# Norm scales made with tokens on partitions and turned by TensorE, wide squares in the gate stages, and a late residual scale

## The chip, the cores and the metric

The kernel runs on one core of one Trainium2 chip. A core has five engines with queues of their own: TensorE (PE in the rows; its weight loads are PEld), VectorE (DVE), ScalarE (ACT), GpSimd (POOL) and SyncE (SP), which here issues the weight transfers. Each works through its own instructions in order and waits on semaphores for the others. The metric is the device time of one execution in microseconds; lower is better.

## The reference, cut to what matters

One call computes two blocks on 256 tokens of width 1024. The first is ffn1, a mixer of two kinds of attention, ffn2 and a final norm. The second has two layers: SSD or retention, then PEER (a lookup among 16384 experts), then a gated embedding ("ple"), and a final norm. What the change touches is the norm in front of each stage; the first block's last norm and the second block's first stand directly one behind the other:

```python
def rms_norm(x, g):
    xf = x.astype(jnp.float32)
    y = xf * lax.rsqrt(jnp.mean(xf * xf, axis=-1, keepdims=True) + EPS)
    return (y * g.astype(jnp.float32)).astype(x.dtype)
...
    return rms_norm(x, final_norm)          # end of the first block
...
    h = x                                   # second block
    for i in range(DEPTH_2):
        hn = rms_norm_2(h, mix_norm[i])
        y = ssd_mixer(hn, ...) if i == 0 else retention(hn, ...)
        h = h + y
        h = h + peer_ffn(rms_norm_2(h, ffn_norm[i]), ...)
        g = jax.nn.sigmoid(rms_norm_2(h, ple_norm[i]) @ ple_gate[i])
        h = h + g * (p[i] @ ple_proj[i])
    return rms_norm_2(h, final_norm)
```

## The kernel before

The activations `x` lie feature-major in SBUF: 128 features on partitions, 8 chunks, 256 tokens. Every large product is made in three matmuls of split fp32 (L323 to L325: high weight by high and by low activation, low weight by high activation). A weight unit of 128x1024 is fetched by a SyncE transfer (L243) into one of three `w` buffers, cast by ScalarE to `wh` (L258) and subtracted by VectorE to `wl` (L260); the transfer for a unit three further on can start when that subtract has freed the buffer. There are three pairs of `wh` and `wl`, and two more are lent in some stages. The products go to four PSUM banks named `mm`, so TensorE can be at most four blocks ahead of whoever reads them.

A norm is made late: the products are taken of the unnormed `x` times its gain (`prep`, L353), and the result of each block is multiplied by `r`, one over the root of the mean square. For each chunk `prep` has ScalarE square `x` (L372) and GpSimd add it into `sqa` (L373). `root` (L401) sums over the partitions with one fp32 matmul of a ones matrix by `sqa` (L405), which leaves the sum on all 128 partitions for 256 tokens; ScalarE takes the root of 128x256 (L407) and `rstd` has VectorE make the reciprocal of 128x256 (L413). Where tokens are on partitions instead (the mixer's and the retention's values), `columns` (L416) turns a row of `r` with two small transposes (L421) and copies it (L423). `scales` (L380) already made such scales with tokens on partitions, for other norms, by one-column matmuls (L387), and `spread` (L394) turned them back with two transposes (L398).

The order on each engine is set by a scheduler from the order of the code. What is wrapped in `later` (L426) is made when first asked for, with a priority of 200 instructions ahead; `blocks` (L475) calls the consumer of a block's bank one block later with the same priority.

At the end of ffn2 two scales are made: `r1` for the first block's last norm, and `r2` for the second block's first norm on top of it, from `sqa` and from `sqb`, the squares times that norm's gain (`both`, L1443; `both_scales`, L1453). SSD's first products are multiplied by `r2` (`cv`, L837). The residual `x` itself must be multiplied by `r1` (L440, eight chunks) before SSD's output is added to it; `settle` (L1458) does so in steps that `ssd` calls between blocks. In the gate stages (`ple`, L1297) the squares come from a loop ahead of it, eight ScalarE squares and seven GpSimd adds.

The stages by the span's microseconds: ffn1 to 196, mixer to 321, ffn2 to 500, SSD to 711, peer0 to 1505, ple0 to 1547, retention to 1745, peer1 to 2539, ple1 to 2574, then the final norm.

## Time and profile before

| | |
|---|---|
| time, median of 3 runs (lowest to highest) | 2590.43 us (2588.69 to 2594.27) |
| the profiled execution | 2587.22 us |
| its span, first to last instruction | 2585.5 us |
| mean granted TensorE clock | 0.993 of full |
| busy: TensorE, VectorE, ScalarE, GpSimd | 98%, 77%, 52%, 7% of the span |

A timeline row gives the start, the time and the engine of one instruction or of a few alike in a row, its line, what it writes and reads, and in brackets how long the engine was idle before it and what ended that. A matmul row counts the records of the profiler: an fp32 matmul leaves two. Matmuls overlap, so the time between the starts of two rows tells what one costs, not the time of a row.

### The profile page before, as it was taken

What the parts mean: (1) busy time and instruction counts of PE and PEld (TensorE: products, weight loads), DVE (VectorE), ACT (ScalarE), POOL (GpSimd) and SP (SyncE); (2) the same over time, 40 slices, a digit from 0 to 9 for tenths busy, and PEclk for the clock granted to TensorE, in tenths of its full rate; (3) what the DMA queues carried; (4) which work ended last, traced back from release to release, by engine and by line L of the source; (5) the groups of instructions that cost most, each with busy time, mean ns of one, the idle gap of its engine ahead of it and who ended that gap; (6) DMA issues with size and microseconds to landing.
All of it is one profiled execution on the core that took longest, in us unless ns stands there. A gap on an engine that the chain in (4) does not pass through costs nothing.

```text
span 2585.5 us, 49071 instructions
## 1 busy us (share of the span) xinstructions
PE 2527.7 (98%) x19798; PEld 2349.4 (91%) x19798; DVE 1991.9 (77%) x3465; ACT 1337.3 (52%) x1824; POOL 191.6 (7%) x216
## 2 busy tenths in 40 slices
PE   8999999998999999999999999999999999999998
PEld 8998899988999999998888889999999999888887
DVE  8766776699789998868865566658999886886555
ACT  6555655587555444444444465555544444444445
POOL 1010100100102120000000030010112000000002
PEclk9999999999999999999999999999999999999999
DMA  6664366654465655555566656555565555556663
GB/s 219 203 193 140 123 197 188 184 204 142 133 192 184 199 180 165 167 176 179 170 189 192 195 182 188 165 167 187 185 194 182 165 167 176 179 171 190 192 193 122
DMA packets 128037, 460.20 MB, mean 178 GB/s; under 512 B 14688, under 2 KB 15424, under 8 KB 127168
## 3 DMA queue, kind: packets, MB, share of 16 engines
q1 hardware_dynamic: 125984, 452.32, 55.8%
q0 software_dynamic: 1536, 4.20, 0.5%
q8 instruction: 155, 2.54, 0.4%
q14 instruction: 74, 0.61, 0.1%
q10 hardware_dynamic: 288, 0.53, 0.1%
HBM read 455.91 MB, written 1.08 MB: 177 GB/s over the span
## 4 chain that ended last, share of the span: by engine, by line
PE 76%; DVE 7%; ACT 2%; issue 1%; POOL 1%; DMA 0%; POOLq 0%; DVEq 0%; ACTq 0%
PE mm L323 14%; PE mm L324 14%; PE mm L325 14%; PE acc L324 9%; PE acc L323 9%; PE acc L325 9%; PE mm L1119 2%; DVE wl L260 2%; DVE eq L1270 1%; DVE f L1273 1%; DVE ca L841 1%; PE pv L325 1%; PE pv L323 1%; PE pv L324 1%; PE sc L1240 1%
## 5 line engine op out<-in xcount | busy, mean ns | idle before, releaser
L258 ACT CAST wh<-w 128x1024 fp32r<-128x1024 f32 x856 | 889.9, 1041 | 1127.7 <-PE mm L324 544.4
L260 DVE TENSOR_TENSOR wl<-w,wh 128x1024 fp32r<-128x1024 f32 x856 | 1047.6, 1225 | 421.5 <-ACT wh L258 419.5
L323 PE MATMUL mm<-ah,wh 128*128 128x256 f32 x3448 | 967.0, 281 | 22.8 <-DVE cv L837 13.8
L325 PE MATMUL mm<-ah,wl 128*128 128x256 f32 x3448 | 962.0, 279 | 8.9 <-DVE wl L260 8.8
L324 PE MATMUL mm<-ah,wh 128*128 128x256 f32 x3448 | 962.7, 279 | 0.4 <-DVE ah L360 0.3
L323 PEld LDWEIGHTS mm<-ah,wh 128*128 128x128 f32 x3448 | 651.2, 189 | 26.2 <-issue 7.5
L325 PEld LDWEIGHTS mm<-ah,wl 128*128 128x128 f32 x3448 | 651.3, 189 | 14.4 <-DVE wl L260 13.9
L324 PEld LDWEIGHTS mm<-ah,wh 128*128 128x128 f32 x3448 | 651.8, 189 | 1.5 <-DVE ah L360 0.8
L324 PE MATMUL acc<-wl,ah 128*128 128x512 f32 x1024 | 402.8, 393 | 0.0
L325 PE MATMUL acc<-wh,ah 128*128 128x512 f32 x1024 | 398.6, 390 | 0.0
L323 PE MATMUL acc<-wh,ah 128*128 128x512 f32 x1024 | 307.0, 391 | 0.0
L323 PEld LDWEIGHTS acc<-wh,ah 128*128 128x128 f32 x1024 | 192.3, 188 | 39.5
L325 PEld LDWEIGHTS acc<-wh,ah 128*128 128x128 f32 x1024 | 192.2, 188 | 38.6
L324 PEld LDWEIGHTS acc<-wl,ah 128*128 128x128 f32 x1024 | 192.5, 188 | 38.2
L373 POOL TENSOR_TENSOR sqa<-sqa,sqt 128x256 f32<-128x256 f32 x82 | 82.7, 1009 | 1669.8 <-ACT sqt L372 1578.4
L1123 DVE TENSOR_TENSOR G<-mm,G 128x512 f32<-128x512 f32 x128 | 88.0, 689 | 49.8 <-PE mm L1119 49.8
L323 PE MATMUL mm<-hh,wh 128*128 128x256 f32 x352 | 97.2, 276 | 0.0
L324 PE MATMUL mm<-hl,wh 128*128 128x256 f32 x352 | 97.2, 276 | 0.0
L325 PE MATMUL mm<-hh,wl 128*128 128x256 f32 x352 | 97.2, 276 | 0.0
L1119 PEld LDWEIGHTS <-two 128*128 128x128 f16 x2048 | 69.8, 97 | 20.2 <-issue 15.9
L1107 DVE TENSOR_TENSOR two<-iota,tabs 128x1024 f16<-128x1024 f16 x128 | 87.3, 682 | 0.0
L1119 PE MATMUL mm<-one,two 128*128 128x64 f16 x2048 | 86.1, 194 | 0.0
(347 smaller groups left out, 3195.7 us busy)
## 6 DMA issues: line engine op xcount, KB each, us to landing
w<-in_peer_u_dram SPq DMA_DIRECT2D x256, 512.0 KB, 3.7
w<-in_peer_v_dram SPq DMA_DIRECT2D x256, 512.0 KB, 4.2
w<-in_ffn_gu_dram SPq DMA_DIRECT2D x88, 512.0 KB, 4.4
w<-in_ssd_in_dram SPq DMA_DIRECT2D x40, 512.0 KB, 4.1
w<-in_ffn_dn_dram SPq DMA_DIRECT2D x32, 512.0 KB, 3.7
w<-in_peer_q_dram SPq DMA_DIRECT2D x32, 512.0 KB, 4.3
w<-in_ssd_out_dram SPq DMA_DIRECT2D x16, 512.0 KB, 3.8
w<-in_ple_g_dram SPq DMA_DIRECT2D x16, 512.0 KB, 3.7
```

Of the source, the lines that this page charges most:

```text
L258: nc.scalar.copy(h[:, :n], w[:, :n])
L260: (nc.gpsimd if own else nc.vector).tensor_tensor(l[:, :n], w[:, :n], h[:, :n].bitcast(FT), OP.subtract)
L323: mm(ps, h, xh, start=start, stop=False, skip_group_check=True)
L324: mm(ps, h, xl, start=False, stop=False, skip_group_check=True)
L325: mm(ps, l, xh, start=False, stop=stop, skip_group_check=True)
L373: (add or nc.gpsimd).tensor_tensor(self.sq[tag], self.sq[tag], t, OP.add)
L841: nc.vector.scalar_tensor_tensor(acc[:, j:], v[:, :S - j], tap(3 - j), acc[:, j:], op0=OP.mult, op1=OP.add)
L1107: nc.vector.tensor_tensor(two, keys.to_broadcast(every), tab[1].to_broadcast(every), OP.is_equal)
L1119: nc.tensor.matmul(ps[:, t, :], two[:, t // 2, :, t % 2], one[i][:, t // 2, :, t % 2], start=i == 0, stop=i == 1)
L1123: nc.vector.tensor_tensor(ga, ps.rearrange("p t e -> p e t"), ga, OP.mult)
L1240: nc.tensor.matmul(ps[:, c * PK:(c + 1) * PK], qT[:, 2 * h + c, t * P:(t + 1) * P], keys[:, c, :], start=True, stop=True)
L1270: nc.vector.tensor_tensor(eq, f[:, c, h, :, None].to_broadcast([P, K, K]), self.iota[:, None, :K].to_broadcast([P, K, K]), OP.is_equal)
```

## The change

`rstd` now takes one or more tiles of squares. For each half of 128 tokens it multiplies the squares, as the stationary operand, by one column of ones, adding the tiles up in PSUM, so that the sums lie with tokens on partitions, two columns wide. Root and reciprocal are taken of 128x2; two transposes spread the result over the other half of the same bank, and VectorE copies 128x256 of it to `r`. The 128x2 tile is kept as `self.rt`, and `columns` is gone. `prep`'s last square is no longer added by GpSimd: it is kept as a second tile ("tail"), so a norm at the mixer, ffn2, peer and the retention has two tiles. In `both` the last chunk's two adds go to VectorE. `r1` is made by `settle`, inside SSD. The gate stage makes its own squares: two ScalarE squares of four chunks each, and two VectorE adds that leave two tiles; its blocks are consumed two later and not one later.

```diff
--- before.py
+++ after.py
@@ -359,9 +359,9 @@
         nc.scalar.activation(h, x, AF.Identity, scale=gc)
         nc.vector.scalar_tensor_tensor(l, x, gc, h.bitcast(FT), op0=OP.mult, op1=OP.subtract)
         if squares:
-            self.square(x, c == 0)
-
-    def square(self, x, first, tag="sqa", scale=1.0, add=None):
+            self.square(x, c == 0, tail=c == KC - 1)
+
+    def square(self, x, first, tag="sqa", scale=1.0, add=None, tail=False):
 
         nc = self.nc
         if first:
@@ -370,6 +370,9 @@
         else:
             t = self.small.tile([P, S], FT, tag="sqt", name="sqt")
             nc.scalar.activation(t, x, AF.Square, scale=scale)
+            if tail:
+                self.sq["tail"] = t
+                return
             (add or nc.gpsimd).tensor_tensor(self.sq[tag], self.sq[tag], t, OP.add)
 
     def near_sqrt(self, after):
@@ -398,30 +401,25 @@
             self.nc.tensor.transpose(ps[:, t * P:(t + 1) * P], c[:, t:t + 1].to_broadcast([P, P]), self.ident)
         return ps[:, :S]
 
-    def root(self, n, sq="sqa", eps=0, tag="r", bank="mm"):
+    def rstd(self, n, *sq, eps=0, tag="r", bank="mm"):
+
 
         nc = self.nc
         ps = self.bank(bank)
-        nc.tensor.matmul(ps[:, :S], self.ones, self.sq[sq], start=True, stop=True)
+        sq = sq or [self.sq[k] for k in ("sqa", "tail") if k in self.sq]
+        self.sq.pop("tail", None)
+        for t in range(NT):
+            for i, q in enumerate(sq):
+                nc.tensor.matmul(ps[:, t:t + 1], q[:, t * P:(t + 1) * P], self.ones[:, 0:1],
+                                 start=i == 0, stop=i == len(sq) - 1)
+        self.rt = c = self.small.tile([P, NT], FT, tag="cols", name="cols")
+        nc.scalar.activation(c, ps[:, :NT], AF.Sqrt, bias=self.vec("eps", eps), scale=1.0 / n)
+        nc.vector.reciprocal(c, c)
+        for t in range(NT):
+            nc.tensor.transpose(ps[:, S + t * P:S + (t + 1) * P], c[:, t:t + 1].to_broadcast([P, P]), self.ident)
         r = self.small.tile([P, S], FT, tag=tag, name=tag)
-        nc.scalar.activation(r, ps[:, :S], AF.Sqrt, bias=self.vec("eps", eps), scale=1.0 / n)
+        nc.vector.tensor_copy(r, ps[:, S:])
         return r
-
-    def rstd(self, *args, **keys):
-
-        r = self.root(*args, **keys)
-        self.nc.vector.reciprocal(r, r)
-        return r
-
-    def columns(self, r):
-
-        nc = self.nc
-        ps = self.bank()
-        for t in range(NT):
-            nc.tensor.transpose(ps[:, t:t + 1], r[0:1, t * P:(t + 1) * P], self.ident[0:1, 0:1])
-        c = self.small.tile([P, NT], FT, tag="cols", name="cols")
-        nc.vector.tensor_copy(c, ps[:, :NT])
-        return c
 
     def later(self, make):
 
@@ -662,7 +660,8 @@
                     for t in range(NT):
                         o = slice(t * P, (t + 1) * P)
                         self.mm3(pv[t], self.xh[:, k, o], self.xl[:, k, o], h[:, w], l[:, w], k == 0, k == KC - 1)
-            rt = self.columns(r())
+            r()
+            rt = self.rt
             mv = [pool.tile([P, 512], FT, name=f"mv{t}") for t in range(NT)]
             for t in range(NT):
                 nc.scalar.activation(mv[t], pv[t], AF.Identity, scale=rt[:, t:t + 1])
@@ -977,7 +976,7 @@
             decay = pool.tile([P, RET_H, NT, S], FT, name="decay")
             nc.sync.dma_start(decay, self.a["ret_decay"])
             turn = self.later(lambda: nc.vector.tensor_tensor(rot, rot, r()[:, None, :].to_broadcast([P, 2, S]), OP.mult))
-            rt = self.later(lambda: self.columns(r()))
+            rt = lambda: r() and self.rt
             yh, yl = pool.tile([P, 16, S], FR, name="yh"), pool.tile([P, 16, S], FR, name="yl")
 
             def rotated(name):
@@ -1294,9 +1293,17 @@
 
 
 
-    def ple(self, l, r, proj, ready):
+    def ple(self, l, proj, ready):
         nc, ws = self.nc, self.ws
         with self.tc.tile_pool(name="ple", bufs=2) as pool:
+            sq = pool.tile([P, KC, S], FT, name="sq", bufs=1)
+            for c in (0, 4):
+                nc.scalar.activation(sq[:, c:c + 4, :], self.x[:, c:c + 4, :], AF.Square)
+            self.near_sqrt(self.x[:, KC - 1, 0:1])
+            for c in (4, 2):
+                nc.vector.tensor_tensor(sq[:, :c, :], sq[:, :c, :], sq[:, c:2 * c, :], OP.add)
+            r = self.later(lambda: self.rstd(D, sq[:, 0, :], sq[:, 1, :]))
+
             def use(d, ps):
                 t = pool.tile([P, S], FT, name="t")
                 nc.vector.tensor_tensor(t, ps[:, :S], r(), OP.mult)
@@ -1309,7 +1316,7 @@
                 ready(d)
 
             ws.pool_every = 0
-            self.blocks(KC, use)
+            self.blocks(KC, use, lag=2)
             ws.pool_every = 0
 
 
@@ -1443,8 +1450,10 @@
             def both(d):
                 if d == 3:
                     self.near_sqrt(self.x[:, d, 0:1])
-                self.prep(d, "final_norm_both")
-                self.square(self.x[:, d, :], d == 0, "sqb", self.vec("final_norm", d))
+                add = nc.vector if d == KC - 1 else None
+                self.prep(d, "final_norm_both", squares=False)
+                self.square(self.x[:, d, :], d == 0, add=add)
+                self.square(self.x[:, d, :], d == 0, "sqb", self.vec("final_norm", d), add)
 
             more = ExitStack()
             pool = more.enter_context(tc.tile_pool(name="both", bufs=1))
@@ -1453,18 +1462,16 @@
             def both_scales():
 
                 nc.vector.scalar_tensor_tensor(sqb, self.sq["sqa"], EPS, sqb, op0=OP.mult, op1=OP.add)
-                return self.rstd(D, "sqb", 1, "r2"), self.root(D, bank="po")
+                return self.rstd(D, sqb, eps=1, tag="r2")
 
             def settle():
-                r1 = two()[1]
-                nc.vector.reciprocal(r1, r1)
+                r1 = self.rstd(D, bank="po")
                 yield
                 for c in range(0, KC, 2):
                     self.scale_residual("final_norm", r1, (c, c + 1))
                     yield
 
-            two = self.later(both_scales)
-            r = lambda: two()[0]
+            r = self.later(both_scales)
             for l in range(2):
                 if l == 0:
                     self.phase_banks(sc=2, po=2)
@@ -1482,16 +1489,12 @@
                 r = self.later(lambda: self.rstd(D))
                 self.phase_banks(sc=4)
                 proj = self.peer(l, r, f"ffn_norm_2{l}", lambda d: self.prep(d, f"ple_norm_2{l}", squares=False))
-                for c in range(KC):
-                    self.square(self.x[:, c, :], c == 0)
-                self.near_sqrt(self.x[:, KC - 1, 0:1])
-                r = self.later(lambda: self.rstd(D))
                 spare = self.lend((self.peer_at + [len(self.ws.units)])[l + 1])
                 if l == 0:
                     more = ExitStack()
                     pool = more.enter_context(tc.tile_pool(name="xparts2", bufs=1))
                     parts = [pool.tile([P, KC, S], FR, name=n) for n in ("bh", "bl")]
-                    self.ple(l, r, proj, lambda d: self.prep(d, f"mix_norm_2{l + 1}", parts))
+                    self.ple(l, proj, lambda d: self.prep(d, f"mix_norm_2{l + 1}", parts))
                     self.xh, self.xl = parts
                     r = self.later(lambda: self.rstd(D))
                 else:
@@ -1505,7 +1508,7 @@
                         if d < 3:
                             nc.scalar.activation(x, x, AF.Identity, scale=self.vec("final_norm_2", d))
 
-                    self.ple(l, r, proj, last)
+                    self.ple(l, proj, last)
             spare.close()
             c = self.scales(D, "sqa", "last")
             two = self.spread(c), self.spread(c)
```

VectorE at the start of SSD, before, from the sum for `r2` to the first product scaled by it (`wl` is a weight subtract, `x` the residual's scaling, `cv` the first reader of an SSD bank):

```order
L1455 SCALAR_TENSOR_TENSOR sqb<-sqa,sqb 128x256
L1460 RECIPROCAL r<-r 128x256
L260 TENSOR_TENSOR wl<-w,wh 128x1024
L440 SCALAR_TENSOR_TENSOR x<-x,vecs,r 128x256
L260 TENSOR_TENSOR wl<-w,wh 128x1024
L440 SCALAR_TENSOR_TENSOR x<-x,vecs,r 128x256 x5
L413 RECIPROCAL r_6294<-r_6294 128x256
L440 SCALAR_TENSOR_TENSOR x<-x,vecs,r 128x256 x2
L260 TENSOR_TENSOR wl<-w,wh 128x1024 x2
L837 TENSOR_TENSOR cv<-mm,r_6294 128x256
```

and the same place after:

```order
L376 TENSOR_TENSOR sqa<-sqa,sqt 128x256
L376 TENSOR_TENSOR sqb<-sqb,sqt 128x256
L1464 SCALAR_TENSOR_TENSOR sqb<-sqa,sqb 128x256
L260 TENSOR_TENSOR wl<-w,wh 128x1024 x2
L417 RECIPROCAL cols<-cols 128x2
L421 COPY r_6312<-mm 128x256
L260 TENSOR_TENSOR wl<-w,wh 128x1024
L836 TENSOR_TENSOR cv<-mm,r_6312 128x256
```

The residual's eight scalings and one weight subtract have moved from in front of the first `cv` to some 80 rows behind it, and the last square's two adds have come in.

ScalarE in ple0, before, from a weight cast (`wh`) through the last squares (`sqt`) to the norm's root:

```order
L258 CAST wh<-w 128x1024
L378 ACT_TABLE_LOAD
L378 ACTIVATE warm<-x,vecs 128x1
L372 ACTIVATE sqt<-x 128x256
L258 CAST wh<-w 128x1024
L372 ACTIVATE sqt<-x 128x256
L258 CAST wh<-w 128x1024
L372 ACTIVATE sqt<-x 128x256 x2
L258 CAST wh<-w 128x1024
L372 ACTIVATE sqt<-x 128x256
L258 CAST wh<-w 128x1024
L407 ACTIVATE r<-mm,vecs 128x256
```

and after:

```order
L258 CAST wh<-w 128x1024
L1301 ACTIVATE sq<-x 128x1024
L381 ACT_TABLE_LOAD
L381 ACTIVATE warm<-x,vecs 128x1
L258 CAST wh<-w 128x1024 x4
L416 ACTIVATE cols<-mm,vecs 128x2
L258 CAST wh<-w 128x1024
```

The squares are done four casts ahead of the root, and the root stands behind those casts.

VectorE in ple0, before, from `prep`'s last rows (`ah`) to the first block scaled by `r`:

```order
L360 SCALAR_TENSOR_TENSOR ah<-x,vecs,ah 128x256 x4
L260 TENSOR_TENSOR wl<-w,wh 128x1024
L360 SCALAR_TENSOR_TENSOR ah<-x,vecs,ah 128x256 x4
L260 TENSOR_TENSOR wl<-w,wh 128x1024 x5
L413 RECIPROCAL r<-r 128x256
L1302 TENSOR_TENSOR t<-mm,r 128x256 x2
```

and after:

```order
L360 SCALAR_TENSOR_TENSOR ah<-x,vecs,ah 128x256 x4
L260 TENSOR_TENSOR wl<-w,wh 128x1024
L1304 TENSOR_TENSOR sq<-sq 128x1024
L260 TENSOR_TENSOR wl<-w,wh 128x1024
L1304 TENSOR_TENSOR sq<-sq 128x512
L260 TENSOR_TENSOR wl<-w,wh 128x1024 x3
L417 RECIPROCAL cols<-cols 128x2
L260 TENSOR_TENSOR wl<-w,wh 128x1024
L421 COPY r<-mm 128x256
L1309 TENSOR_TENSOR t<-mm,r 128x256 x2
```

The adds have come in between the subtracts, and the copy of `r` stands one subtract behind the reciprocal. On TensorE, L405 stood after 48 of the stage's 192 matmuls; after, in ple0, the one-column matmuls stand after 71 and the transposes after 72, in ple1 after 61 and 72.

## Rows read from the trace of the kernel before

**Rows 1.** Page, first part: TensorE's busy time, share of the span, instructions.

```profile
PE 2527.7 (98%) x19798; PEld 2349.4 (91%) x19798; DVE 1991.9 (77%) x3465; ACT 1337.3 (52%) x1824; POOL 191.6 (7%) x216
```

**Rows 2.** TensorE's waits: us in total, times, longest us.

```profile
PE mm L323 <- DVE cv L837: 13.8, 5, 5.4
...
PE mm L405 <- POOL sqa L373: 7.7, 2, 4.4
...
PE po L889 <- DVE y L893: 4.1, 1, 4.1
```

**Rows 3.** Windows: stretch, length, busy us of PE, PEld, DVE, ACT, POOL, clock, DMA.

```profile
513.00:517.00 4.00, 3.90 (x18) 3.90 (x19) 3.23 (x11) 3.82 (x8) 0.00 (x0) 0.50 0.64 247
517.00:521.00 4.00, 4.00 (x32) 4.00 (x32) 2.03 (x6) 3.96 (x6) 0.00 (x0) 0.85 0.00 0
600.00:620.00 20.00, 16.72 (x148) 16.05 (x147) 19.95 (x41) 17.58 (x36) 0.00 (x0) 1.00 0.60 184
```

**Rows 4.** Timeline of TensorE round an L405 (start us, us, engine, line, operation).

```profile
500.48 0.28 PE L325 MATMUL mm<-ah,wl 128*32 128x256 f32 x1
500.60 0.59 PE L405 MATMUL po<-sqa,ones 128*128 128x256 f32 x2
...
501.15 0.28 PE L325 MATMUL mm<-ah,wl 128*128 128x256 f32 x1
```

**Rows 5.** Timeline of TensorE round one-column matmuls L387.

```profile
240.70 0.28 PE L324 MATMUL mm<-ah,wh 128*128 128x256 f32 x1
240.82 0.50 PE L387 MATMUL po<-ones,sqq 128*128 128x1 f32 x4
...
241.39 0.28 PE L323 MATMUL mm<-ah,wh 128*128 128x256 f32 x1
```

**Rows 6.** Timeline of TensorE round the transposes L398.

```profile
582.94 0.28 PE L325 MATMUL mm<-ah,wl 128*128 128x256 f32 x1
583.06 0.38 PE L398 MATMUL sc<-ident,col 128*128 128x128 f32 x2
...
583.40 0.28 PE L324 MATMUL mm<-ah,wh 128*128 128x256 f32 x1
```

**Rows 7.** Timeline of TensorE round the small transposes L421.

```profile
224.09 0.39 PE L325 MATMUL sc<-wh,ah 128*128 128x512 f32 x1
224.41 0.28 PE L421 MATMUL mm<-ident,r 1*128 1x1 f32 x2
...
224.84 0.28 PE L324 MATMUL mm<-ah,wh 128*128 128x256 f32 x1
```

**Rows 8.** Timeline of VectorE at the start of SSD.

```profile
503.41 1.16 DVE L260 TENSOR_TENSOR wl<-w,wh 128x1024 fp32r<-128x1024 f32 x1
...
506.02 2.06 DVE L440 SCALAR_TENSOR_TENSOR x<-x,vecs,r 128x256 f32<-128x256 f32 x5
508.00 1.74 DVE L413 RECIPROCAL r<-r 128x256 f32<-128x256 f32 x1
...
512.63 0.41 DVE L837 TENSOR_TENSOR cv<-mm,r 128x256 f32<-128x256 f32 x1
```

**Rows 9.** Timeline of ScalarE at the start of SSD.

```profile
504.90 1.05 ACT L258 CAST wh<-w 128x1024 fp32r<-128x1024 f32 x1 [0.93 <-PE mm L324]
```

**Rows 10.** Timeline of ScalarE in ple0.

```profile
1512.73 1.28 ACT L378 ACT_TABLE_LOAD   x1
...
1521.47 1.04 ACT L258 CAST wh<-w 128x1024 fp32r<-128x1024 f32 x1 [0.65 <-DMA w<-in_ple_g_dram]
```

**Rows 11.** Timeline of TensorE in ple0 and ple1, at the norm's matmul.

```profile
1522.40 1.22 PE L405 MATMUL mm<-sqa,ones 128*128 128x256 f32 x2 [4.40 <-POOL sqa L373]
1523.06 0.78 PE L323 MATMUL mm<-ah,wh 128*128 128x256 f32 x1
...
2555.00 0.70 PE L405 MATMUL mm<-sqa,ones 128*128 128x256 f32 x2 [3.33 <-POOL sqa L373]
```

**Rows 12.** Timeline of VectorE in ple0.

```profile
1515.60 1.25 DVE L260 TENSOR_TENSOR wl<-w,wh 128x1024 fp32r<-128x1024 f32 x1 [0.42 <-ACT wh L258]
```

## The prediction

> **What bounds the kernel now.** I read the page's first part, then the TensorE's list of waits, then the timelines at the longest of these waits. TensorE is busy 98% of the span [rows 1], so outside a few stretches any instruction added to TensorE costs its issue time and work taken from other engines costs nothing. The exceptions stand in the list of waits [rows 2]: 13.8 us for the first consumers of SSD's matmul banks (VectorE's `cv`, the longest 5.4), 7.7 in two waits of the norm's L405 for GpSimd's last square, and 4.1 for SSD's `y`. In the middle of SSD, from 600 to 620, VectorE is busy 19.95 of 20 us [rows 3]: there, and only there, VectorE sets the time. So the change can win in SSD and in the two gate stages (ple0 near 1520 us, ple1 near 2553), and must pay everywhere else.
>
> **Part 1: norm scales with tokens on partitions (all sites).** Before, a norm costs TensorE one ones-by-squares matmul. From the L325 at 500.48 to the one at 501.15 is 0.67 us and holds two ordinary steps of 0.113: L405 adds 0.44 [rows 4]. After, it is a one-column matmul per token tile and square tile and then two transposes. Both forms exist already. Four one-column records make 0.69 of two ordinary steps: +0.46 [rows 5]. Two transposes make 0.46 of two steps: +0.23 [rows 6]. The kernel's entry to ffn1 has one square tile (0.46 + 0.23 - 0.44 = +0.25). The entries to the mixer, ffn2, peer0, the retention and peer1 have two, `sqa` and the unadded last square: 2 x 0.46 + 0.23 - 0.44 = +0.71 each, 5 x 0.71 = +3.55. TensorE has no wait of note at these five, so GpSimd's last add and VectorE's 1.7 us reciprocal, both removed, hid behind queued matmuls; removing them saves nothing there. The dropped `columns` had two small transposes at two sites. From the L325 at 224.09 to the L324 at 224.84 is 0.75 for steps worth 0.33 [rows 7]: -0.42 each, -0.84 together. The new small steps stand in queues. At the mixer, VectorE's copy of `r` follows two weight subtracts of 1.2 us [rows 8] while TensorE has 14 matmuls (1.6 us) until it needs a bank; I add 0.4 for the mixer and peer0 together (bounds 0 and 1). Sum of part 1: 0.25 + 3.55 - 0.84 + 0.4 = **+3.4**.
>
> The Trainium skill ("TensorE: Matmul & The Clock Gate", section "Back-to-back issue gap") would price the one-column matmul lower: about 60 cycles for up to 64 columns, some 25 ns, when it stands alone. By it the five sites would cost 5 x (0.2 + 0.23 - 0.44), about nothing, and the forecast would be 3.6 us lower. The row decides against it: 0.46 us for four records, each of which has a 128-column weight load to itself.
>
> **Part 2: SSD's start and the late residual scale.** Before, VectorE runs a reciprocal for `r1`, six scalings L440 between weight subtracts, a second reciprocal of 1.74 us at 508.00, two scalings and two subtracts, and reaches the first `cv` at 512.63 [rows 8]. TensorE has run out of banks 5.4 us earlier and restarts at half clock: 513 to 517 is granted 0.50 and holds 18 matmuls where 35 fit [rows 3], some 2.5 us with the edges. So 8 us of TensorE's time hang on that `cv`. After, in front of it stand three 128x256 adds, three subtracts instead of four, a 128x2 reciprocal and one copy. The third subtract decides: its cast waits for TensorE to free a buffer, as it did at 504.90 before [rows 9]; TensorE comes there some 0.4 earlier without `r1`'s L405, so cast to 505.5, subtract to 506.7, `cv` near 506.7. That is 6.0 us earlier and before the banks run out; this stall and its half clock go.
>
> Part of it is given back, because the middle of SSD is VectorE's. Work that stood ahead of the first `cv` now stands behind: eight scalings (5 in 2.06 us [rows 8], 3.2), `r1`'s small reciprocal and copy (0.5) and one subtract (1.2), in all 4.9. Against that, VectorE waited for the half-speed TensorE behind `cv`: it was busy 3.23 and 2.03 of the four microseconds from 513 and from 517 [rows 3], so 2.7 us idle, which go with the half clock. Net at the end of SSD: -6.0 + 4.9 - 2.7 = -3.8. ScalarE gets a Sqrt table load and a reload inside SSD (1.28 each [rows 10]). ScalarE is not the bound there, but its `zt` and `ct` feed VectorE. Bounds: all 8 gained; or, with both loads in VectorE's way, -6.0 + 4.9 + 2.6 = +1.5. I take **-3.8**, nearest to the row that shows VectorE full.
>
> **Part 3: the gates' squares.** Before, seven GpSimd adds follow one another, TensorE issues two blocks (48 matmuls) and waits 4.40 us at L405, until 1522.40. It restarts at 1523.06 with 144 matmuls left, at half clock: the L405 pair took 1.22 us, against 0.59 at 500.60 [rows 4, 11]. After, two wide squares and two VectorE adds, estimated by casts and subtracts of that width, have the sum ready near 1518.4, and L413 stands after 71 matmuls. But the transposes stand one matmul later and need the reciprocal. ScalarE's Sqrt is behind four weight casts, where only one cast came between the last squares and the Sqrt before; the fourth is the trouble. Its buffer is refilled when the subtract three units earlier is over. Before, such a subtract ended at 1516.85 and the cast waiting for that DMA began at 1521.47, 4.6 us later [rows 10, 12]. After, a 128x1024 add stands in front of that subtract, so it ends near 1517.8, the cast runs from 1522.0 to 1523.0 and the Sqrt follows. Then VectorE does a subtract, the reciprocal, another subtract that waits for its own DMA, and only then the copy that frees the bank: near 1526.1 (subtracts of 1.2 us and, for the second, a refill that began near 1519.6). So the stall is not removed but moved, from 1517.9 to 1522.4 before, to 1520.9 to 1526.1 after. TensorE restarts 3.05 us later with 24 matmuls fewer (2.72), and at half clock again: **+0.5** (bounds: -3.5 if the Sqrt comes before the transposes are reached, and +2). In ple1 the order is alike, with 72 matmuls before the transposes. TensorE restarted at about 2555.3 before [rows 11]; the same chain of refill, cast, Sqrt, subtract, reciprocal, subtract, copy ends near 2559.5, 4.2 later for 2.7 fewer: **+1.6** (bounds -2 and +3).
>
> **Sum.** 3.4 - 3.8 + 0.5 + 1.6 = +1.7 us against the profiled execution, 2587.22 (span 2585.5 and 1.7 around it): 2588.9. The profiled one lies 3.2 below the median of the three runs, 2590.43; on the median's scale, 2592.1. What a measurement here can tell from no change is about 0.2%, 5.2 us.
>
> **Rivals.**
>
> A. The gate stalls close. If the refills land a little earlier than I count, the Sqrt is done before TensorE reaches the transposes: ple0 -3.5, ple1 -2. For it: the sum is ready almost two microseconds before TensorE asks for it, and GpSimd's chain is gone. Against it: the cast order, in which one late DMA holds the Sqrt. With my SSD term this is 3.4 - 3.8 - 3.5 - 2 = -5.9, 2584.5; with SSD's whole 8 us, 2580.3.
>
> B. SSD gives everything back, slower. Its place is VectorE's full stretch in the middle of SSD: 4.9 us of moved work and two table loads in ScalarE's queue ahead of VectorE's operands. It decides as soon as these cost more than the 6.0 us by which `cv` is earlier. The price is -6.0 + 4.9 + 2.6 = +1.5 in place of -3.8; with the gates as I have them 3.4 + 1.5 + 0.5 + 1.6 = +7.0, 2597.4, and with the gates at their upper bounds 2600.3. For it: 19.95 of 20 us. Against it: the idle behind `cv` at half clock, which must shrink.
>
> C. The small matmuls cost what the page says and not what the row says: 2588.5. It changes no sign; 2 in 100.
>
> D. The change does not do what it says, since `cv` still comes after the banks run out: the third subtract then waits for a weight that lands later, near 508 as before. Then 2 to 3 us of the stall and the half clock stay, SSD is about 0, and the time is 2595.9; 8 in 100.
>
> **How the numbers follow.** My forecast has 48 in 100, C 2, D 8, A 22, B 20. Forecast, C and most of D lie within 0.2% (2585.2 to 2595.6), with some edge on both sides. Faster: A and 4 of the forecast's edge, 0.26. Slower: B, half of D and a little edge, 0.26. Same: 0.48. The likeliest is 2592.1, its own range 2588 to 2596. The range for 8 in 10 goes half into A and half into B: 2582.5 to 2599.
>
> **What will show it.** Right: the first `cv` between 506 and 507.5 with no TensorE wait of over 1 us in front; the list of waits without L405's GpSimd waits but with L419 or the next matmul waiting 4 to 6 us in each gate stage, ended by a reciprocal or the copy of `r`; five places with about 0.7 us more on TensorE; and SSD's end 3 to 5 us earlier against its start. Wrong: a gate stage without a wait of over 2 us (A); SSD no shorter although the stall at 507 is gone (B); `cv` after 508 (D). My forecast also falls if the change lengthens the transfer waits elsewhere, which I count at nothing because the weight stream's order outside these stages is the same.

## The result

The changed kernel takes 2610.01 us (median of 4 runs, 2607.61 to 2612.04) against 2589.56 for the kernel before, run beside it: a ratio of 1.0076 [1.0058, 1.0093]. It is slower by 20 us, outside the predicted range. The profiled execution took 2608.58 us, with a span of 2606.8 against 2585.5: 21.3 us to find.

The page of the changed kernel, its span and its first part (busy us, share, instructions), against [rows 1]:

```profile
span 2606.8 us, 49173 instructions
PE 2546.6 (98%) x19862; PEld 2367.6 (91%) x19862; DVE 1985.1 (76%) x3479; ACT 1334.5 (51%) x1812; POOL 168.7 (6%) x195
```

TensorE is busy 19 us longer. So most of the loss isn't waiting, and the list of TensorE's waits in the changed kernel (us in total, times, longest), which answers to [rows 2], agrees:

```profile
PE mm L325 <- DVE wl L260: 8.5, 18, 1.0
PE mm L323 <- DVE r L421: 7.7, 4, 2.7
...
PE mm L323 <- DVE cv L836: 5.8, 3, 3.2
PE sc L875 <- DVE bc L844: 5.7, 2, 3.1
PE mm L419 <- DVE cols L417: 3.7, 2, 2.3
PE po L888 <- DVE e L884: 2.6, 1, 2.6
PE po L888 <- ACT ca L838: 2.0, 1, 2.0
```

The norm's waits for GpSimd (7.7) are gone but for 0.5, and `cv` fell from 13.8 to 5.8; waits for `r`, for the 128x2 tile `cols` and for other operands of SSD have come.

To see where the time went, I took the start of the k-th split matmul (L323 to L325; both kernels have 17028) in both traces and subtracted. The last of them starts 20.78 us later, gained in these stages (each taken from a moment just ahead of its norm to the same moment of the next; in the trace of before 193, 317, 500, 1548 and 2551 us, and 716 behind peer0's entry):

| stage | forecast | changed kernel |
|---|---|---|
| ffn1 | +0.25 | +2.73 |
| mixer | +0.5 | +1.19 |
| ffn2 | +0.7 | **+10.94** |
| SSD (with peer0's entry) | -2.9 | +3.54 |
| peer0, ple0 | +0.5 | -1.18 |
| retention, peer1 | +1.0 | +1.31 |
| ple1 | +1.6 | +2.25 |

ffn2 is the largest, and TensorE never waits in the middle of it. Windows of the kernel before and of the changed kernel there (stretch, length, busy us and instructions of PE, PEld, DVE, ACT, POOL, granted clock, DMA share, GB/s):

```profile
340.00:480.00 140.00, 140.00 (x1238) 140.00 (x1237) 92.81 (x120) 72.99 (x107) 7.00 (x8) 1.00 0.64 192
```

```profile
340.00:480.00 140.00, 140.00 (x1169) 140.00 (x1168) 89.24 (x117) 67.08 (x99) 3.54 (x4) 1.00 0.58 180
```

Both are full and granted 1.00, the upper of the two levels, yet the second holds 69 matmuls fewer: 140/1238 is 113 ns a step, 140/1169 is 120. TensorE's timeline of the changed kernel shows where the step changes:

```profile
327.83 0.28 PE L325 MATMUL mm<-ah,wl 128*128 128x256 f32 x1
327.95 0.28 PE L323 MATMUL mm<-ah,wh 128*128 128x256 f32 x1
328.06 0.38 PE L419 MATMUL mm<-ident,cols 128*128 128x128 f32 x2
328.20 0.37 PE L324 MATMUL mm<-ah,wh 128*128 128x256 f32 x1
...
328.64 0.28 PE L323 MATMUL mm<-ah,wh 128*128 128x256 f32 x1
328.76 0.28 PE L324 MATMUL mm<-ah,wh 128*128 128x256 f32 x1
328.88 0.28 PE L325 MATMUL mm<-ah,wl 128*128 128x256 f32 x1
329.00 0.28 PE L323 MATMUL mm<-ah,wh 128*128 128x256 f32 x1
```

Up to the pair of transposes (L419) starts lie 0.11 to 0.12 apart in turn (113 ns), behind it 0.12 each time, and so on to 514 us. I counted the steps of 118 to 122 ns among all 13,500 steps between split matmuls of 128x256: 1591 before, 3593 after. The 2002 more, at 6.67 ns each (120.0 less 113.3), are **13.4 us** of the 21.3.

The other places follow. In ffn1 VectorE's timeline shows the reciprocal done early and the copy of `r` late, behind four operations that build a table; TensorE's shows who waited:

```profile
23.12 0.16 DVE L417 RECIPROCAL cols<-cols 128x2 f32<-128x2 f32 x1
...
28.13 1.95 DVE L592 SCALAR_TENSOR_TENSOR alibi<-dist,mask 128x384 f32<-128x384 f32 x4
30.00 0.41 DVE L421 COPY r<-mm 128x256 f32<-128x256 f32 x1
```

```profile
30.57 0.35 PE L323 MATMUL mm<-ah,wh 128*128 128x256 f32 x1 [2.15 <-DVE r L421]
```

In the gate stages TensorE stops twice where it stopped once before [rows 11], first for `cols`, then for `r`, in ple0 and ple1:

```profile
1538.19 0.95 PE L413 MATMUL mm<-ones,sq 128*128 128x1 f32 x8
...
1541.70 0.54 PE L419 MATMUL mm<-ident,cols 128*128 128x128 f32 x2 [2.34 <-DVE cols L417]
...
1544.56 0.58 PE L323 MATMUL mm<-ah,wh 128*128 128x256 f32 x1 [2.32 <-DVE r L421]
```

```profile
2575.23 0.43 PE L419 MATMUL mm<-ident,cols 128*128 128x128 f32 x2 [1.38 <-DVE cols L417]
...
2578.39 0.58 PE L323 MATMUL mm<-ah,wh 128*128 128x256 f32 x1 [2.73 <-DVE r L421]
```

In SSD the first `cv` stands at 521.54; less the 14.86 us by which the stage starts late that is 506.7, 5.9 earlier than in [rows 8], and TensorE waits only 0.52 there. Beside the kernel before it has won 7.2 us since the stage's start by the matmul that stood at 520 there, and has lost them again by the one at 550. Further on it waits twelve times for 0.7 to 3.2 us. The half clock has moved: from 500 to 720 us these are the windows of 20 us in which the granted clock is short of 1.00, in the kernel before and in the changed one:

```profile
500.00:520.00 20.00, 14.60 (x103) 14.24 (x102) 16.81 (x30) 11.62 (x17) 0.07 (x1) 0.83 0.39 126
...
640.00:660.00 20.00, 15.18 (x103) 13.11 (x102) 18.48 (x36) 16.14 (x34) 0.00 (x0) 0.74 0.33 102
```

```profile
540.00:560.00 20.00, 14.04 (x107) 12.58 (x106) 13.50 (x24) 14.60 (x31) 0.00 (x0) 0.89 0.65 235
560.00:580.00 20.00, 18.06 (x143) 17.07 (x143) 18.24 (x41) 18.29 (x36) 0.00 (x0) 0.94 0.54 185
580.00:600.00 20.00, 16.16 (x125) 15.82 (x125) 19.89 (x41) 11.78 (x20) 0.00 (x0) 0.91 0.59 185
...
660.00:680.00 20.00, 17.33 (x135) 14.40 (x135) 19.97 (x40) 13.76 (x31) 0.00 (x0) 0.83 0.23 74
```

The shortfalls add up to 0.43 of a window in either kernel. In the first of the four VectorE is not full (13.50 of 20 us). It stands idle behind ScalarE, and TensorE behind it:

```profile
550.01 0.42 DVE L844 SCALAR_TENSOR_TENSOR bc<-ct,ca 128x256 f32<-128x256 f32 x1 [4.67 <-ACT ct L843]
```

```profile
553.95 0.67 PE L875 MATMUL sc<-bc 128*128 128x256 f32 x2 [3.10 <-DVE bc L844]
```

That `ct` stands in ScalarE's queue behind twelve operations on `cums` (cumulative sums that SyncE fetches into SBUF), and ScalarE was idle for 5.45 us before these. The transfer was issued at 538.26 and landed 7.1 us later, when they began (the profile puts the wait down to a `cv` that ended in the same 0.1 us; with part 2 alone, below, it names the transfer).

SSD's +3.54 holds 399 more steps of 120 ns (2.7 us) and the 0.7 of peer0's entry. What is left is about nothing, where -3.8 was forecast.

### The profile page after: what moved, and what is told of

It is laid out like the page before. It is cut to its first block, busy times and chain, and to the rows that moved or that the text cites. A ratio compares the mean times of both kernels' runs of the same rounds, so it can differ in the third digit from the quotient of the medians.

```text
span 2606.8 us, 49173 instructions
## 1 busy us (share of the span) xinstructions
PE 2546.6 (98%) x19862; PEld 2367.6 (91%) x19862; DVE 1985.1 (76%) x3479; ACT 1334.5 (51%) x1812; POOL 168.7 (6%) x195
## 4 chain that ended last, share of the span: by engine, by line
PE 88%; DVE 7%; ACT 2%; DMA 2%; issue 1%; POOL 0%; POOLq 0%; DVEq 0%; ACTq 0%; SPq 0%
PE mm L323 18%; PE mm L324 17%; PE mm L325 17%; PE acc L324 9%; PE acc L323 9%; PE acc L325 9%; PE mm L1118 2%; DVE wl L260 2%; DVE eq L1269 1%; ACT wh L258 1%; DVE f L1272 1%; PE pv L325 1%; PE pv L323 1%; PE sc L1239 1%; PE pv L324 1%
## 5 line engine op out<-in xcount | busy, mean ns | idle before, releaser
L323 PE MATMUL mm<-ah,wh 128*128 128x256 f32 x3448 | 968.4, 281 | 23.4 <-DVE r L421 7.7
L325 PE MATMUL mm<-ah,wl 128*128 128x256 f32 x3448 | 963.0, 280 | 8.5 <-DVE wl L260 8.5
L323 PEld LDWEIGHTS mm<-ah,wh 128*128 128x128 f32 x3448 | 650.0, 189 | 28.3 <-ACT wh L258 9.4
L325 PEld LDWEIGHTS mm<-ah,wl 128*128 128x128 f32 x3448 | 650.2, 189 | 13.3 <-DVE wl L260 12.9
L325 PE MATMUL acc<-wh,ah 128*128 128x512 f32 x1024 | 398.6, 390 | 0.0
L323 PE MATMUL acc<-wh,ah 128*128 128x512 f32 x1024 | 307.0, 391 | 0.0
L323 PEld LDWEIGHTS acc<-wh,ah 128*128 128x128 f32 x1024 | 192.3, 188 | 39.5
L325 PEld LDWEIGHTS acc<-wh,ah 128*128 128x128 f32 x1024 | 192.3, 188 | 38.5
L376 POOL TENSOR_TENSOR sqa<-sqa,sqt 128x256 f32<-128x256 f32 x62 | 62.5, 1008 | 564.3 <-ACT sqt L372 477.2
L323 PE MATMUL mm<-hh,wh 128*128 128x256 f32 x352 | 98.3, 279 | 0.0
L325 PE MATMUL mm<-hh,wl 128*128 128x256 f32 x352 | 98.3, 279 | 0.0
L1118 PEld LDWEIGHTS <-two 128*128 128x128 f16 x2048 | 69.8, 97 | 20.2 <-issue 15.9
```

What stands on the lines that cost most here:

```text
L323: mm(ps, h, xh, start=start, stop=False, skip_group_check=True)
L325: mm(ps, l, xh, start=False, stop=stop, skip_group_check=True)
L376: (add or nc.gpsimd).tensor_tensor(self.sq[tag], self.sq[tag], t, OP.add)
L1118: nc.tensor.matmul(ps[:, t, :], two[:, t // 2, :, t % 2], one[i][:, t // 2, :, t % 2], start=i == 0, stop=i == 1)
```

## The experiments

Theory after these traces: the small matmuls of the new scale switch the stream from 113 to 120 ns a step, and this costs 13 us. Rivals: the stream is slower for another reason in the change (other places of tiles, other work beside it), and the loss is mostly the new waits. The first four kernels add small transposes to the kernel before, undo part 1, alter the group of small matmuls, and make part 1 alone. Times of the kernel before beside them: 2586.88 us.

**Two transposes in the kernel before**, directly behind each norm's matmul; their result is not used.

```diff
         nc.tensor.matmul(ps[:, :S], self.ones, self.sq[sq], start=True, stop=True)
+        for t in range(NT):
+            nc.tensor.transpose(ps[:, S + t * P:S + (t + 1) * P], self.ones[:, t:t + 1].to_broadcast([P, P]), self.ident)
```

> The kernel before, with two transposes of a column of ones (written where nothing reads them) put directly behind each ones-by-squares matmul; nothing else of the change. Theory P (pace): transposes leave the stream of split matmuls behind them at 120.0 ns per step instead of 113.3 until the stream is broken, so ffn2 runs at 120 (+11 us there), and the time is 2600 to 2605. Rival L (something else of the change slows ffn2: the unadded square tile, the moved small tiles, another load of the other engines): ffn2 stays at 113.3 and the time is 2590 to 2594, 7 x 0.23 us more than before.

2590.17 us, 1.0012 [1.0002, 1.0022]; ffn2's window holds 1238 matmuls, as under rival L. Slow steps are 1975; the 384 more than before lie nearly all in SSD. So transposes as such don't slow the stream: here they stand in one group with the two records of L405.

**The changed kernel with the old scales**: one matmul with the ones per tile of squares, root and reciprocal of 128x256, `columns` again; the rest as changed.

```diff
-        for t in range(NT):
-            for i, q in enumerate(sq):
-                nc.tensor.matmul(ps[:, t:t + 1], q[:, t * P:(t + 1) * P], self.ones[:, 0:1], ...)
...
-            nc.tensor.transpose(ps[:, S + t * P:S + (t + 1) * P], c[:, t:t + 1].to_broadcast([P, P]), self.ident)
+        for i, q in enumerate(sq):
+            nc.tensor.matmul(ps[:, :S], self.ones, q, start=i == 0, stop=i == len(sq) - 1)
```

> The changed kernel with the ones-by-squares matmul (one per square tile), root and reciprocal of 128x256 and the small transposes put back; the unadded last square, the wide squares of the gate stages and the late residual scale stay. P: ffn2 at 113.3, ffn1's 2.2 us wait for the copy of r gone, time 2590 to 2596. L: ffn2 still at 120, time 2603 to 2608.

2590.25 us, 1.0014 [1.0004, 1.0024]; 1238 matmuls in ffn2's window, 1771 slow steps. Nearly the whole loss goes with part 1. ffn1 is +0.25, SSD still +2.9, and ple1 is now -2.34.

**Columns behind the pair**: in the changed kernel, two more one-column matmuls (four records) follow each pair of transposes.

```diff
             nc.tensor.transpose(ps[:, S + t * P:S + (t + 1) * P], c[:, t:t + 1].to_broadcast([P, P]), self.ident)
+        for t in range(NT):
+            nc.tensor.matmul(ps[:, NT + t:NT + t + 1], sq[0][:, t * P:(t + 1) * P], self.ones[:, 0:1], ...)
```

> The changed kernel with four one-column records (the sums once more, into two columns that nothing reads) behind the two transposes of each norm. P, in the form that what stands last before the stream sets its pace, and that one-column records leave it fast as they do in both traces: ffn2 at 113.3, about 13 us less for 9 x 0.46 us more, time 2598 to 2602. P, in the form that any transposes in the neighbourhood are enough, and L: ffn2 at 120, time 2611 to 2615.

2596.97 us, 1.0037 [1.0025, 1.0049]: more work, and 10 us over the kernel before beside it, where the changed kernel was 20 over. ffn2's window holds 1238, slow steps are 1694, though ffn1's wait for `r` grew from 2.15 to 4.2 us (ffn1 is +6.5). What the pair does to the stream is undone by what follows it.

**Part 1 alone** in the kernel before: `rstd`, `self.rt` and the tail, with both scales made together as before and the old gate squares.

> The kernel before with part 1 alone: the new scales and the unadded last square, with the gates' squares in the old loop and the residual's scale made beside the other at SSD's start. P: ffn2 at 120, ffn1's wait for the copy of r as in the changed kernel, so 13 + 3 + 2 us over the kernel before, 2604 to 2610. Rival Q (the slower pace comes from parts 2 or 3, by another order of the whole program): ffn2 at 113.3, 2592 to 2597.

2609.46 us, 1.0097 [1.0076, 1.0118]; 1169 in ffn2's window, 3643 slow steps, ffn1 +2.68. Part 1 is the loss, and the pace is most of it. ple0 is +3.7 here, where the new scale's chain stands behind GpSimd's adds.

These four leave open whether it is the number of small matmuls in the group. The next four were run beside a kernel before of 2587.99 us.

**Four transposes for two in the changed kernel**, everywhere: the pair is issued twice.

```diff
-        for t in range(NT):
+        for t in (0, 1, 0, 1):
             nc.tensor.transpose(ps[:, S + t * P:S + (t + 1) * P], c[:, t:t + 1].to_broadcast([P, P]), self.ident)
```

> The changed kernel with each norm's pair of transposes issued twice into the same place (four in a row, the second pair repeats the first). Theory G (group): a group of exactly two narrow matmuls in the stream leaves it at 120 ns per step, a group of four leaves it at 113.3 (in the traces so far four one-column or four transposed records were followed by 113 in all but a few per cent, pairs by 120 in most). So ffn2 at 113.3, 9 x 0.23 us more records, time 2596 to 2600. Rival H: it is the transposes as such, or what waits around them; ffn2 at 120, time 2611 to 2614.

2607.26 us, 1.0077 [1.006, 1.0094]: the time expected did not come, the pace did. ffn2's window holds 1238 and slow steps fall to 1483, 14 us less; but SSD came out 7 us longer than in the changed kernel (+10.3; why is open), and ffn1's longest wait for `r` grew to 3.5.

**Two, and four, transposes in the kernel before, as a group of their own**, once `r` is finished, 24 to 55 split matmuls behind the norm's matmul (46 in ffn2). Their result is not used.

```diff
+        for t in range(NT):                # in the second kernel: for t in (0, 1, 0, 1)
+            self.nc.tensor.transpose(self.upper[:, S + t * P:S + (t + 1) * P], r[:, t:t + 1].to_broadcast([P, P]), self.ident)
```

> The kernel before with two transposes of the finished r, some 46 matmuls behind the ones-by-squares matmul, as a group of their own, into the free half of its bank (nothing reads them). G: ffn2 at 120 ns per step (+10 us) and the mixer's first products too (+1 us), time 2600 to 2605. Rival K (the one-column matmuls of the sum are needed for the slow pace): ffn2 at 113.3, time 2590 to 2594.

> As the run before, at the same place in the stream, with four transposes in a row instead of two. G: ffn2 at 113.3, time 2591 to 2595, below the pair although it issues more. H: ffn2 at 120, 2602 to 2607. K: 113.3.

Two: 2608.77 us, 1.008 [1.0059, 1.01]. Four: 2590.04, 1.0012 [1.0003, 1.0022]. With two the time lies above the 2600 to 2605 expected: ffn1 was switched to 120 as well (+9.9 us), which was not foreseen, and the mixer was not. With four it is a little under the 2591 to 2595 expected. The windows of ffn1 and ffn2 with two, then with four:

```profile
40.00:195.00 155.00, 155.00 (x1294) 155.00 (x1293) 104.93 (x144) 78.84 (x116) 10.22 (x9) 1.00 0.62 190
340.00:480.00 140.00, 140.00 (x1169) 140.00 (x1169) 91.20 (x119) 66.72 (x100) 2.76 (x3) 1.00 0.60 185
```

```profile
40.00:195.00 155.00, 155.00 (x1370) 155.00 (x1369) 110.67 (x150) 83.31 (x121) 10.43 (x11) 1.00 0.67 204
340.00:480.00 140.00, 140.00 (x1238) 140.00 (x1237) 93.56 (x119) 72.80 (x109) 7.04 (x8) 1.00 0.65 192
```

TensorE's timeline of the kernel with two, at the pair in ffn2, and of the kernel with four:

```profile
338.17 0.38 PE L415 MATMUL mm<-ident,r 128*128 128x128 f32 x2
...
338.63 0.28 PE L324 MATMUL mm<-ah,wh 128*128 128x256 f32 x1
338.75 0.28 PE L325 MATMUL mm<-ah,wl 128*128 128x256 f32 x1
338.87 0.28 PE L323 MATMUL mm<-ah,wh 128*128 128x256 f32 x1
```

```profile
327.97 0.60 PE L415 MATMUL mm<-ident,r 128*128 128x128 f32 x4
...
328.99 0.28 PE L324 MATMUL mm<-ah,wh 128*128 128x256 f32 x1
329.10 0.28 PE L325 MATMUL mm<-ah,wl 128*128 128x256 f32 x1
329.21 0.28 PE L323 MATMUL mm<-ah,wh 128*128 128x256 f32 x1
```

This is the cleanest pair of runs: same kernel, same code place, nobody uses the result, and twice the work is 19 us cheaper. Slow steps are 4641 with two and 1605 with four: 3036 x 6.67 ns = 20.2 us.

**Part 2 alone** in the kernel before: `r1` made in `settle`, the last chunk's adds on VectorE.

```diff
-                return self.rstd(D, "sqb", 1, "r2"), self.root(D, bank="po")
+                return self.rstd(D, "sqb", 1, "r2")
...
-                r1 = two()[1]
-                nc.vector.reciprocal(r1, r1)
+                r1 = self.rstd(D, bank="po")
```

> The kernel before with part 2 alone: r1 made inside SSD by the old root and a reciprocal of 128x256, and the last chunk's adds on VectorE; the norms and the gates as before. My step: the first cv comes 4 to 6 us earlier, the stall of 5.4 us at 507 and its half clock go, and the end of SSD gains 3 to 4 us: 2583 to 2586. Rival B (SSD gives it back in VectorE's full stretch): the stall goes and new ones of the same sum stand between 520 and 670, 2586 to 2591.

2587.64 us, 1.000 [0.999, 1.001]. VectorE's timeline, ScalarE's, and two of TensorE's waits:

```profile
506.21 1.16 DVE L260 TENSOR_TENSOR wl<-w,wh 128x1024 fp32r<-128x1024 f32 x1
507.29 0.41 DVE L837 TENSOR_TENSOR cv<-mm,r 128x256 f32<-128x256 f32 x1
```

```profile
529.93 4.26 ACT L855 ACTIVATE e<-cums,tok 128x256 f32<-128x256 f32 x12 [3.68 <-DMA cums<-sums]
```

```profile
PE mm L323 <- DVE cv L837: 6.0, 6, 2.8
PE mm L323 <- DVE z L901: 4.5, 1, 4.5
```

`cv` comes 5.3 us earlier and its waits fall from 13.8 to 6.0, and SSD as a whole is 1.3 us longer: all is given back, as in rival B. TensorE has won 7.9 us since the stage's start by the matmul that stood at 520 before, and by the one at 550 nothing is left. ScalarE's wait for `cums` has come; the kernel before has none there.

The last four test part 3, the price of the pair in the kernel before itself, and the repair. The kernel before beside them: 2587.76 us.

**Part 3 alone**: the gates' squares in two wide operations, two adds and two tiles, users two blocks behind; the scale stays the old one, with two ones matmuls.

```diff
-            self.blocks(KC, use)
+            self.blocks(KC, use, lag=2)
...
+            for c in (0, 4):
+                nc.scalar.activation(sq[:, c:c + 4, :], self.x[:, c:c + 4, :], AF.Square)
...
+            r = self.later(lambda: self.rstd(D, [sq[:, 0, :], sq[:, 1, :]]))
```

> The kernel before with the third part alone: the gates' squares in blocks of four chunks, their sums folded on VectorE, two matmuls with the ones over both halves, the users two blocks behind; the scales stay as they were (square root and reciprocal on 128x256). Theory that the stages' sizes carry over from the kernel that had all but the new scales: first gate +0.5 us, second gate -2.3 us, so about 1.8 us under the kernel before, and TensorE's waits for GpSimd's sums (4.40 and 3.33 us) gone. Rival, by my own sum for this part: the waits only move to the scale's next link, first gate +0.5 and second gate +1.6 less the 0.7 us of new records each, so within 1 us of the kernel before.

2584.69 us, 0.9997 [0.9986, 1.0007]. ple0 +0.1, ple1 -2.8 us. TensorE's waits in ple0:

```profile
1522.20 0.38 PE L323 MATMUL mm<-ah,wh 128*128 128x256 f32 x1 [1.45 <-ACT r L409]
...
1526.16 0.38 PE L323 MATMUL mm<-ah,wh 128*128 128x256 f32 x1 [0.95 <-DVE t L1312]
```

With the old scale 2.4 us of waits are left there, with the new one 4.66. The sizes are near those expected; the whole is too small to tell from no change.

**Four transposes at the last retention head**, in the kernel before. A lone pair stood there already.

```diff
-        for t in range(NT):
+        for t in list(range(NT)) * times:
...
-                rr = self.spread(c, "sc")
+                rr = self.spread(c, "sc", 2 if h == RET_H - 1 else 1)
```

> The kernel before; only the spreading of the last retention head's scale issues its two transposes twice, four in a row. Theory that a lone pair leaves the stream of 128x256 matmuls at 120 ns a step and four leave it at 113.3: the slow stretch behind that pair (about 380 steps from 1702 to 1746 us) runs at 113.3, 380 x 6.67 ns = 2.5 us less, and 0.2 us more for two transposes: 2.3 us under the kernel before. Rival, that this stretch is slow for another reason (the weights read there, or the place): it stays at 120 ns and the time is that of the kernel before, or 0.2 us more.

2585.6 us, 0.9996 [0.9987, 1.0004]. The windows behind that pair, before and with four:

```profile
1703.00:1746.00 43.00, 43.00 (x359) 42.95 (x358) 26.45 (x40) 20.90 (x35) 8.17 (x9) 1.00 0.53 166
```

```profile
1703.00:1746.00 43.00, 43.00 (x380) 42.95 (x379) 28.55 (x42) 22.67 (x36) 7.97 (x9) 1.00 0.53 166
```

The stretch was slow and is not any more: retention and peer1 are 2.1 us shorter (2.3 expected). Kernels with nothing changed there (part 2 and part 3 alone) came out at -0.4 and -0.6, so the windows are the firmer figure. The whole time alone could not show it.

**Both together.**

> The third part alone and the four transposes in the last retention head together. If both theories hold, the sums add: 1.8 + 2.3, about 4 us under the kernel before. If only one holds, about 2 us under; if neither, no difference.

2583.77 us, 0.9988 [0.9979, 0.9997]: the medians differ by the 4 us expected (3.1 by the ratio), and this is the one kernel of the study that is faster than the one before by more than its interval, if only just.

**The repair**: the changed kernel, with four transposes in the scales of the mixer and ffn2 only.

```diff
-            r = self.later(lambda: self.rstd(D))
+            r = self.later(lambda: self.rstd(D, times=2))
```

> The changed kernel; the pair of transposes is issued twice, four in a row, in the scales of the mixer and of the second feed-forward stage alone (the order elsewhere stays that of the changed kernel). Theory that the pair's pace is what the change lost: 202 to 228 and 329 to 514 us run at 113.3 ns a step, some 1780 steps x 6.67 ns = 11.9 us less, and 0.5 us more for the two pairs: about 11 us under the changed kernel, 10 us over the kernel before (2598). Rival, that the stages behind give back what is gained there, as the changed kernel with four transposes everywhere did: second feed-forward stage 10 us shorter, but the stages behind 10 us longer, no more than 3 us under the changed kernel.

2597.4 us, 1.0043 [1.003, 1.0057], where 2598 was expected. It is 9.6 us over the kernel before beside it, where the changed kernel was 20.4 over: 10.8 us less (11 expected), and slow steps are 1732, 1861 fewer or 12.4 us. So the pace's share of the loss is shown by time as well. Some 10 us stay: ffn1 +2.4, SSD +2.9, ple1 +1.6 and small entries.

## Why the prediction was wrong

**What bounds the kernel.** That "any instruction added to TensorE costs its issue time": here the prediction failed. It priced each small matmul by the gap it opens, and took the stream around it to be the same before and after, a term put at nothing. It measured +13.4 us, 2002 more slow steps: the stream has two steps at the same granted clock, and a pair of transposes by itself can switch it for the next 180 us. The trace of before showed it: 359 records in 43 us behind the pair at 1701.59, where 380 fit, and the pair of [rows 6] itself stands in a stream of 120 ns, which four transposes of SSD's own at 580.71 had started. I read the price of the pair from those rows and not the pace of the stream around it.

**Part 1, +3.4.** The terms of issue were about right: the four one-column records at 516.03 of the changed kernel add 0.46 us to the stream, as in [rows 5], and the retention and peer1, which have no new wait, are +1.31 for +1.0 forecast. That figure is loose: kernels without a new instruction there came out at -0.4 and -0.6, and the slow steps there are 97 fewer than before. The missing term is the pace, +13.4. The second miss is ffn1: +0.25 forecast, +2.73 measured, by one wait. I had allowed 0.4 for the copy at the mixer and peer0 and none at ffn1, where VectorE was building tables. A copy behind the transposes is a new link that needs VectorE late, and its place in VectorE's queue is what it costs. As a whole part 1 alone is some +20 us in the traces, 22.6 by the medians. The Trainium skill ("TensorE: Matmul & The Clock Gate", section "Back-to-back issue gap") says that the spacing in a stream is set by the weight loads and the matmuls together; no run here takes the two apart, and the steps measured were 113.3 and 120.0 ns.

**Part 2, -3.8.** `cv` came where it was forecast (507.29 alone, 506.7 in the changed kernel), and the stall there went. What failed is the net. The sum let the half clock and VectorE's idle time go (-2.7); they moved. It also took all of SSD to follow `cv`, and the transfer of `cums` did not: less the start of the stage it was issued only 1.0 us earlier in the changed kernel and 1.6 with part 2 alone, where `cv` came 5 to 6 us earlier. ScalarE, and what stands behind it, then waited. Such a wait of ScalarE, of 3.0 to 5.5 us, is in six of the seven kernels that hold part 1 or 2 and in none of the other seven; the seventh (columns behind the pair) has an SSD 2.2 us shorter than before. So SSD at +1.3 alone and about 0 in the changed kernel is rival B by the price (+1.5, given 20 in 100) and not by the way, since VectorE was not full where the gain was lost. The share of this wait is read from the rows and is not shown by a run that takes it away. One trace of SSD is loose, too: kernels in which SSD is untouched (part 3 alone, the four transposes at the last retention head, and both together) lie between -1.1 and +1.9, and those with part 2 between -2.2 and +10.3.

**Part 3, +0.5 and +1.6.** ple0 -0.8, ple1 +2.25. The stall moved to `cols` and `r`, as forecast: two waits in each gate, 4.66 and 4.11 us together, where one of 4 to 6 was forecast. The sizes can't be told closer: with part 2 alone ple0, untouched, came out at -1.0, and ple1, untouched, at +1.15 in the kernel with four transposes at the last retention head. That it is the new scale's chain and not the squares is shown for ple1 by part 3 alone: -2.8 there.

**Rivals.** A did not come, since the waits stayed. The Trainium skill's price for one-column matmuls ("TensorE: Matmul & The Clock Gate", "Back-to-back issue gap"), rival C, would have made the retention and peer1 about -0.4, as an estimate from its figure; +1.31, and the 0.46 us of the four records at 516.03, speak against it. D did not come either, with `cv` at 506.7. None of the four was what decided, a pace that changes far from the instruction that was added; beyond a sentence on transfers I had kept no chance for a cause outside the places I had sums for.

## What to carry to other kernels

When a change puts small matmuls into a long stream, compare the number of records in equal full windows before and after: busy time and granted clock can both be full while the step differs. Look for the same form in the trace that is there and read the pace behind it, not only the gap it opens. Move a long operation off an engine only with a look at what the added links queue behind, for 1.7 us saved on a reciprocal no one waited for bought a copy that TensorE did wait for.

## What the runs showed of the hardware

A stream of split fp32 matmuls of 128x256 ran at 113.3 or at 120.0 ns a step, at a granted clock of 1.00 in both. Two 128x128 transposes as a group of their own switched it from 113 to 120 in ffn2 in every kernel that had such a pair there; four in a row in the norm's scale never did at ffn1, mixer or ffn2.

What else switches it is not settled. With the late pair the step changed at 25.8, 338.2 and 1548.7 us, where TensorE went from the matmul ahead of the pair to the one behind in 0.25 us; it did not at 210.0, 736.2, 1770.0 and 2580.3, where it took 0.55 us or more and the stream stood still beside the pair. A wait of TensorE ended the slow step, too: in ffn1 the changed kernel's pair at 23.72 switched the stream to 120, and behind the wait at 30.57 it is at 113. It is not transposes alone: in the changed kernel two one-column records at 196.35 switched it from 113 to 120, and behind six at 198.01 it went back. Four are not always harmless: in the kernel before, SSD's own four transposes at 580.71 and 623.87 switched it from 113 to 120. And a pair that meets a stream at 120 can end it (732.2, 1570.9 and 1765.4 in the changed kernel) or leave it (583.06 and 626.34 in the kernel before). What inside TensorE holds the step is not shown by any run here.
